# Down-weight sums of two pairs per layer, moved into the chunks by seven products; the order at the up-projections' ends

## The chip, the cores and the metric

One core of one Trainium2 chip. The metric is the device time of one execution, in microseconds; the kernel before has a median of 1107.97 us over three runs. Engines are named as in the profile: PE (TensorE), DVE (VectorE), ACT (ScalarE), POOL (GpSimd), SP (SyncE, which here only issues DMAs).

## The reference

A trunk of two layers over 512 positions of width 1024, all in float32:

```python
# layer 0: dilated attention, then the gated ConvFFN; one shared K, V and forget gate from the result
# layer 1: forgetting attention (FoX) over the shared K, V, then the gated ConvFFN
def conv_ffn(xn, w_up, cw, cb, w_down):
    a = xn @ w_up                         # 512 x 1024 times 1024 x 5632
    ap = jnp.pad(a, ((0, 0), (CONV_W - 1, 0), (0, 0)))
    a = sum(ap[:, j:j + T] * cw[j] for j in range(CONV_W)) + cb
    gate, val = jnp.split(a, 2, axis=-1)
    return (jax.nn.gelu(gate, approximate=True) * val) @ w_down   # 512 x 2816 times 2816 x 1024
```

## The kernel before

Every float32 product is made of three matmuls (`mm3`, L292 to L294: high by high, high by low, low by high). So each weight tile is needed as a pair: the high part is a rounding copy on ACT, the low part is the rest, by a subtraction on DVE or by a DMA that adds on POOL's queue. All instructions of an engine run in the order in which the program issues them.

**The course.** Attention of layer 0 to about 141 us, its output projection (141 to 182), ConvFFN of layer 0 (to 511), shared keys and values (511 to 611), FoX attention (611 to 727), its output projection (727 to 766), ConvFFN of layer 1 (764 to about 1100). The output projections are followed by a `Boundary`: for each block of 128 positions it normalises the product, adds it to the residual `h` (L337, L342, L344), normalises the sum for the next stage (L309) and transposes it (L360).

**ConvFFN, the up-projection.** 22 chunks c = 0..21 of 128 gate and 128 value columns. Chunks 3 to 20 (`SEVEN`) make their 2 x 2 block product by seven products instead of eight (a Strassen-like scheme): in order P1 = S2, P2 = S3, P3 = A12, P4 = S1, P5 = A22, then P0 = A11 of the next chunk (`open_seven`, its copy is L1002), P6 = S4. Each product is 12 matmuls of 256 columns. The weights of a chunk are made by a generator `seven_weights`, one part at each call of `step`: g0 and g1 the pair `a` (A11; L742, L744, then the adding DMA L745), g2 and g3 the pair `b` (A12 and A22; L748, L750, L751), g4 the sums on DVE and the high part of `u` (S2 and S1; L758, L759, L762), g5 that of `v` (S3 and S4; L764, L766), g6 and g7 the low parts of `u` and `v` (L771, L774). In chunk c, the chunk m = c+1 gets g4 to g7 and n = c+2 gets g0 to g3. After the products come the combining operations on the PSUM banks (copies L1028 `u2`, L1033 `s7`; additions L1038, L1042, L1043), and the convolution's taps (L678 on ACT, L682 on DVE), GELU (L706) and the gate's product (L701 on POOL, stored by L703). Chunks 2 and 21 take plain weights (`plain_weights`: L60 and L62 on ACT).

**Buffers.** The pool `t8` has 16 slots of 8 KB per partition, `t4` has 10 slots of 4 KB. A new tile takes a slot when the slot's last reader has finished. While the chunks by seven products run, 8 slots of `t8` hold the activations (`xsh`, `xsl` and the sums), the other 8 the pairs `a`, `b`, `u`, `v` of chunks c, m and n. `b` of chunk c is last read by P5, `u` by P4, `v` by P6.

**The down-projection.** 11 pairs of 256 rows. For each pair the kernel forms sums of the four quarters of the down weights and keeps them in DRAM (`dT`): `down_sums` loads a pair by three DMAs on SP (L642 to L644, 1 MB), makes four subtractions of 128 x 512 on DVE (L647 to L650) and stores 1 MB (L655). The sums of most pairs are made at other places, with these four among them: layer 0 pair 10 and layer 1 pair 8 in layer 0's output projection (from the function `late` and in the `Boundary`), layer 1 pair 10 in layer 1's output projection (`bd.beside`), and layer 1 pairs 9, 0 and 1 in the stage of the shared keys and values (`down1`). At the end of the up-projection the first pairs of the down-projection are prepared: `pair_sums(j)` (three DVE operations L809 to L811 on the gated activations, a store on POOL L812), `pair_highs(j)` (three ACT copies L819), `pair_lows(j)` (three DVE subtractions L824).

Of the kernel before, what the change touches and what calls it, by code (L numbers as in the profile page):

```python
# [13 lines left out]
ALU = mybir.AluOpType  # L14
# [7 lines left out]
NF = DFF // 128  # L22
# [5 lines left out]
SEVEN = tuple(range(3, 21))  # L28
# [80 lines left out]
def trunk_kernel(ctx, tc, x, norm_gains, w_qkv_a, w_o_a, w_q_b, w_o_b, kv_norm, w_kvf, b_f,  # L109
# [319 lines left out]
    class Boundary:  # L429
# [6 lines left out]
        def __init__(self, gain_mix, gain_next, name):  # L436
            self.mix, self.gain_next, self.name = Mix(gain_mix), gain_next, name
            self.xn, self.r, self.pts = {}, {}, {}
            self.xT, self.beside = None, iter(())

        def half(self, i, n, hf, o):
            b = self.order[i]
            self.mix.half(b, n, hf, o)
            if n == 0:
                if i >= 2:
                    self.transpose(self.order[i - 2])
                if i >= 1:
                    self.norm(self.order[i - 1])
                if i >= 2:
                    self.keep(self.order[i - 2])  # L450
                next(self.beside, None)
            else:
                self.mix.add(b)

# [177 lines left out]
    def down_sums(pairs, place, queue, lag, behind):  # L632


        live, n = [], len(pairs)
        for i in range(n + lag + behind):
            if i < n:
                l, j = pairs[i]
                a, b = place()
                live.append((a, b))  # L640
                r = w_down[l][j * 256:j * 256 + 256, :].rearrange("(c p) d -> c p d", p=128)
                sp.dma_start(a, r[0])  # L642
                sp.dma_start(b[:, 0:512], r[1, :, 512:1024])
                sp.dma_start(b[:, 512:1024], r[1, :, 0:512])  # L644
            if 0 <= i - lag < n:
                a, b = live[i - lag]
                dve.tensor_tensor(a[:, 0:512], a[:, 512:1024], a[:, 0:512], ALU.subtract)  # L647
                dve.tensor_tensor(a[:, 512:1024], b[:, 0:512], a[:, 512:1024], ALU.subtract)
                dve.tensor_tensor(b[:, 0:512], b[:, 0:512], a[:, 0:512], ALU.subtract)
                dve.tensor_tensor(b[:, 512:1024], b[:, 512:1024], b[:, 0:512], ALU.subtract)  # L650
            i -= lag + behind
            if i >= 0:
                l, j = pairs[i]
                for q, t in enumerate(live[i]):
                    queue[min(i, len(queue) - 1)].dma_start(dT[l][j, :, q * 1024:q * 1024 + 1024], t)  # L655
            yield

    def in_one():
# [13 lines left out]
    def ffn(l, bd, cp, nxt, ahead):  # L672
# [112 lines left out]
        def step(c, n=1):  # L785

            if c >= NF or c < 0:
                return
            if c not in gens:
                gens[c] = (seven_weights if c in SEVEN else plain_weights)(c)  # L790
            for _ in range(n):
                next(gens[c], None)
# [193 lines left out]
        step(S0, 4)  # L986
        for _ in split_sums():
            pass
        step(S0, 2)
        post(0, first[0:2])  # L990
        step(S0, 2)
        begun = opened = half_taps = None
        before = 1, first[2:4]

        def prod(o, w, x, start=False):
            half_mm(o, w, x[0:2], x[2], start)
# [8 lines left out]
        for c in range(2, NF):  # L1005
            if c == NF - 4:
                pair_load(0)
            m, n = c + 1, c + 2
            if c in SEVEN:
                x21, x22 = [(xT[0][i], xT[1][i], s) for i, s in ((1, LO), (1, HI))]  # L1010
                banks, s1 = opened
                opened = None
                w = halves.pop(c)
                W.n_get += 2
                o1, o2, o3, o4 = banks[0][:, LO], banks[0][:, HI], banks[1][:, LO], banks[1][:, HI]
                u2, s7 = (t2([128, 256], name="csum") for _ in range(2))
                prod(o2, w.pop("S2"), (*XB, HI))
                prod(o3, w.pop("S3"), (*XA, HI), True)
                product()
                bb = half_taps or t4([128, 2, T], name="bb")  # L1020
                cb, prev = before
                for i, ch in ((1, NF + cb), (0, cb)):
                    if i == 0 or half_taps is None:
                        first_tap(bb, i, prev[i], ch)
                        other_taps(bb, i, prev[i], ch)
                half_taps = None
                step(n)
                act.copy(u2, o2)  # L1028
                step(n)
                prod(o1, w.pop("A12"), x21)  # L1030
                prod(o2, w.pop("S1"), (*XA, LO))
                glu(cb, bb)
                act.copy(s7, o3)  # L1033
                if m in SEVEN:
                    step(m, 2)
                if n in SEVEN:
                    step(n)
                dve.tensor_tensor(o1, o1, s1, ALU.add)  # L1038
                if m in SEVEN:
                    step(m)  # L1040
                prod(o3, w.pop("A22"), (*XB, LO))
                dve.tensor_tensor(o4, o2, s7, ALU.add)  # L1042
                dve.tensor_tensor(o3, o3, u2, ALU.add)  # L1043
                if n in SEVEN:
                    step(n)
                half_taps = t4([128, 2, T], name="bb")
                first_tap(half_taps, 1, banks[1], NF + c)
                if m in SEVEN:
                    opened = open_seven(m)
                    step(m)  # L1050
                else:
                    begun = W.get(), bank([128, T], name="up")
                    up(*begun, range(4))
                    XA.clear()
                    XB.clear()
                    step(m)
                    pair_highs(0)
                    pair_sums(1)
                other_taps(half_taps, 1, banks[1], NF + c)
                prod(o2, w.pop("S4"), x22)  # L1060
            else:
                banks = [bank([128, T], name="up") for _ in range(2)]
                for s in range(2):
                    if s == 0 and begun:
                        w, banks[0] = begun
                        up(*begun, range(4, KD))
                        begun = None
                    else:
                        up(W.get(), banks[s], range(KD))
                    if s == 0 and m in SEVEN:  # L1070
                        opened = open_seven(m)
                        step(n, 2)
                    if s == 0:
                        post(*before, (lambda: pair_lows(0)) if c == NF - 1 else None, half_taps)
                        half_taps = None
                        if c >= NF - 2:
                            pair_highs(c - NF + 2)
                            pair_sums(c - NF + 3)
                    if n not in SEVEN:
                        step(n, 2 - s)  # L1080
                    elif s == 1:
                        step(n, 2)
            before = c, banks
            if c == NF - 3:
                pair_sums(0)
        post(*before, lambda: pair_lows(1))
        pair_highs(2)
        pair_sums(3)
        pair_lows(2)
# [360 lines left out]
    combine(1, 1)  # L1450
    weigh(2, 1)

    beside = down_sums([(0, ND - 1), (1, 8)], in_one, [sp], 2, 2)
    next(beside)
    next(beside)
    rows = load_conv(0)
    grow = t2([16, 128], name="g_rows")
    sp.dma_start(grow[0:8, :], kv_norm.rearrange("(k p) -> k p", p=128))
# [4 lines left out]
    def late():  # L1463
        combine(2, 0)
        combine(2, 1)
        cp.append(conv_columns(rows))
        pg = bank([128, 16], name="g_ps")
        pe.transpose(pg, grow, ident[:16, :16])
        dve.tensor_copy(gcol, pg)
        next(beside)  # L1470
        next(beside)

    bd = Boundary(load_gain(norm_gains[0, 1], "gain01"), load_gain(norm_gains[0, 2], "gain02"), "xb")
    bd.beside = beside
    Proj(6, 4, lambda kc: (OT[kc // 2][:, 0, kc % 2, :], OT[kc // 2][:, 1, kc % 2, :])).finish(bd, 4, late)


# [260 lines left out]
        keep_values(1, 2 + bp, vb[bp])  # L1738
        keep_values(1, bp, vd[bp])
    del w22, S4  # L1740
    down1 = down_sums([(1, j) for j in (9, 0, 1)], in_two, [pool, pool, sp], 1, 1)
    next(down1)
    W.ahead = 2
    W.split(W.n_split + 1)
    for bp in range(2):
# [4 lines left out]
                mm3(vc[bp], ah, al, w4[s][0][:, k, :], w4[s][1][:, k, :], False, False, True)  # L1750
        keep_values(0, bp, vc[bp])
    del w4
    next(down1)
    for c in range(4, 8):
        if c == 7:
            for i in range(4):
# [146 lines left out]
            W.split(W.n_get + 1)  # L1903
    f_bias(0, 0)
    f_bias(0, 1)
    M = len(pairs)
    sums, idle = {}, itertools.repeat(None)
    for j, m in ((2, 2), (3, 6), (4, 10), (5, 14)):
# [49 lines left out]
    W.ahead, W.ahead_dma = 4, 2  # L1958
    cp = conv_columns(load_conv(1))
    bd = Boundary(load_gain(norm_gains[1, 1], "gain11"), load_gain(norm_gains[1, 2], "gain12"), "xc")  # L1960
    bd.beside = down_sums([(1, ND - 1)], in_one, [sp], 1, 1)
    next(bd.beside)
    po.finish(bd, 4)


# [43 lines left out]
```

## Time and profile before

| | before |
|---|---|
| runs | 1106.59, 1108.63, 1107.97 us; median 1107.97 |
| the profiled execution | 1108.61 us, span 1106.8 us, mean granted clock 0.999 |
| busy in the span | PE 1086.2 us (98%), DVE 902.4 (82%), ACT 751.1 (68%), POOL 303.5 (27%) |
| moved by DMA | 250.02 MB, mean 226 GB/s |

A row of the timeline gives an instruction's start and duration in us, its engine and line, and in brackets the idle time of the engine just before it and what ended that. A row of the waits gives how long an engine stood idle for one kind of releaser in all, how many times, and the longest.

### The profile page before, as it was taken

The page shows a single profiled execution, that of the slowest core. Times are in us where ns is not written, and L with a number is a line of the kernel's source. Part 1 is how long each engine was busy: PE and PEld are TensorE (multiplying, and loading weights), DVE is VectorE, ACT ScalarE, POOL GpSimd, SP SyncE. Part 2 cuts the span into 40 slices and gives each one's busy share as a digit, 9 for nine tenths or more (in the row PEclk, how much of TensorE's full clock was granted, in tenths as well). Part 3 has the DMA queues.
Part 4 walks back from the last instruction along what each step waited for, and adds up shares of the span by engine and source line. Part 5 has one row for each costly group of instructions (what it writes and reads, how often), then busy time and mean ns, then how long its engine had stood idle before and what let it go on. Part 6 is the DMA issues. An engine that isn't in the chain of part 4 may idle for free. (4 is left out here: it accounts for less than half of the span.)

```text
span 1106.8 us, 19977 instructions
## 1 busy us (share of the span) xinstructions
PE 1086.2 (98%) x7184; PEld 964.4 (87%) x7184; DVE 902.4 (82%) x1494; ACT 751.1 (68%) x1290; POOL 303.5 (27%) x407
## 2 busy tenths in 40 slices
PE   9999999999999999999999899999999999999997
PEld 6988879999999988887987678788999999997886
DVE  5677788788888889997888677938789888879995
ACT  6644577688787766576554577756777887856573
POOL 4633010232333322000110566610133333321000
PEclk9999999999999999999999999999999999999999
DMA  9589997588888869793774676597688888879862
GB/s 315 128 287 408 372 271 192 130 216 206 210 214 209 212 218 367 264 339 77 210 176 128 192 234 204 156 306 198 144 195 216 210 203 208 214 216 354 313 248 76
DMA packets 192426, 250.02 MB, mean 226 GB/s; under 512 B 13696, under 2 KB 133496, under 8 KB 191816
## 3 DMA queue, kind: packets, MB, share of 16 engines
q1 hardware_dynamic: 169864, 180.81, 50.7%
q0 software_dynamic: 22464, 67.94, 27.2%
q8 instruction: 56, 0.92, 0.3%
q14 instruction: 42, 0.34, 0.1%
HBM read 170.28 MB, written 39.63 MB: 190 GB/s over the span
## 5 line engine op out<-in xcount | busy, mean ns | idle before, releaser
L292 PE MATMUL up<-xsh,w 128*128 128x256 f32 x576 | 163.2, 283 | 1.0 <-ACT csum L1002 1.0
L293 PE MATMUL up<-xsl,w 128*128 128x256 f32 x576 | 163.0, 283 | 0.0
L294 PE MATMUL up<-xsh,w 128*128 128x256 f32 x576 | 163.0, 283 | 0.0
L682 DVE SCALAR_TENSOR_TENSOR bb<-up,conv,bb 128x511 f32<-128x511 f32 (+1 forms) x160 | 119.3, 748 | 14.5 <-ACT bb L678 11.6
L292 PE MATMUL acc<-w 128*128 128x512 f32 (+1 forms) x311 | 120.5, 388 | 0.0
L294 PE MATMUL acc<-w 128*128 128x512 f32 (+1 forms) x311 | 120.4, 387 | 0.0
L292 PEld LDWEIGHTS up<-xsh,w 128*128 128x128 f32 x576 | 110.6, 192 | 1.4 <-ACT csum L1002 1.4
L293 PEld LDWEIGHTS up<-xsl,w 128*128 128x128 f32 x576 | 110.6, 192 | 0.1
L294 PEld LDWEIGHTS up<-xsh,w 128*128 128x128 f32 x576 | 110.6, 192 | 0.0
L293 PE MATMUL acc<-w 128*128 128x512 f32 (+1 forms) x267 | 103.7, 388 | 1.8 <-DVE w L824 1.8
L678 ACT ACTIVATE bb<-up,conv 128x512 f32<-128x512 f32 x80 | 62.1, 779 | 41.3 <-PE up L294 28.8
L751 POOL DMA_DIRECT2D w<-wraw x36 | 30.9, 858 | 166.9 <-ACT w L750 164.8
L60 ACT CAST w<-wraw 128x1024 fp32r<-128x1024 f32 x64 | 66.8, 1053 | 12.4 <-DMA wraw<-in_w_o_b_dram 4.2
L701 POOL TENSOR_TENSOR hc<-bb 128x512 f32<-128x512 f32 x44 | 68.9, 1567 | 0.1
L292 PEld LDWEIGHTS acc<-w 128*128 128x128 f32 x311 | 58.4, 188 | 12.0
L294 PEld LDWEIGHTS acc<-w 128*128 128x128 f32 x311 | 58.4, 188 | 11.8
L69 DVE TENSOR_TENSOR w<-wraw,w 128x1024 fp32r<-128x1024 f32 x44 | 54.3, 1243 | 10.7 <-ACT w L60 8.8
L762 ACT CAST w<-wsum 128x1024 fp32r<-128x1024 f32 x36 | 38.0, 1054 | 36.8 <-DVE wsum L759 36.8
L293 PEld LDWEIGHTS acc<-w 128*128 128x128 f32 x267 | 50.1, 188 | 13.5 <-DVE w L824 3.6
L292 PE MATMUL up<-xbh,w 128*128 128x256 f32 (+1 forms) x176 | 53.6, 304 | 0.5 <-ACT csum L1028 0.3
L292 PE MATMUL up<-xch,w 128*128 128x256 f32 (+1 forms) x176 | 53.5, 304 | 0.5 <-DVE up L1042 0.2
L824 DVE TENSOR_TENSOR w<-wraw,w 128x1024 fp32r<-128x1024 f32 x44 | 54.0, 1268 | 0.0
(344 smaller groups left out, 3476.5 us busy)
## 6 DMA issues: line engine op xcount, KB each, us to landing
wraw<-in_w_up_dram SPq DMA_DIRECT2D x144, 256.0 KB
w<-wraw POOLq DMA_DIRECT2D x56, 512.0 KB, 5.9
dT<-dsums SPq DMA_DIRECT2D x32, 512.0 KB
hD<-hc POOLq DMA_DIRECT2D x44, 256.0 KB, 5.0
dact<-hD SPq DMA_DIRECT2D x44, 256.0 KB
wraw<-dT SPq DMA_DIRECT2D x22, 512.0 KB
wraw<-in_w_down_dram SPq DMA_DIRECT2D x22, 512.0 KB
dsums<-in_w_down_dram SPq DMA_DIRECT2D x18, 512.0 KB
```

The source lines that it names most:

```text
L60: self.nc.scalar.copy(pair[:, 0, s], raw[:, s])
L69: self.nc.vector.tensor_tensor(pair[:, 1, s], raw[:, s], pair[:, 0, s].bitcast(F32), ALU.subtract)
L292: pe.matmul(o, ah, bh, start=first, stop=False, skip_group_check=shared)
L293: pe.matmul(o, ah, bl, start=False, stop=False, skip_group_check=shared)
L294: pe.matmul(o, al, bh, start=False, stop=last, skip_group_check=shared)
L678: act.activation(bb[:, i, :], ps, AF.Identity, bias=cp[:, 3, ch:ch + 1], scale=cp[:, 2, ch:ch + 1])
L682: dve.scalar_tensor_tensor(bb[:, i, n:], ps[:, :T - n], cp[:, 2 - n, ch:ch + 1], bb[:, i, n:], ALU.mult, ALU.add)
L701: pool.tensor_tensor(hc[c], bb[:, 0, :], bb[:, 1, :], ALU.mult)
L751: pool.dma_start(b[:, 1], r1, accum_op=ALU.add)
L762: act.copy(u[:, 0], sb)
L824: dve.tensor_tensor(w[:, 1], r, w[:, 0].bitcast(F32), ALU.subtract)
```

## The change

- `down_sums` of the pairs (0,10), (1,8) and (1,10) go from the output projections; the `Boundary` has no `beside` any more. `down1` makes two pairs, (1,0) and (1,1), instead of three, is begun later (after the last products of the shared values), and its last step comes after the first two biases of FoX.
- In each ConvFFN, a new generator `sums_beside` makes the sums of pairs (l,10) and (1,8+l). It is advanced once in each chunk by seven products, right ahead of the addition L1038: chunk 3 nothing, chunk 4 the three loads into one `t8` tile, chunks 5 to 8 one subtraction each, chunk 9 one store of 1 MB; then the same from chunk 10 to 15.
- The order of other steps: g0 to g3 of chunk 4 are made ahead of the loop, right behind the split of the activations' sums; where chunk n is not by seven products, its weights come after the copy `u2`; g2 (the copy L748 of `b`) stands behind P5 instead of ahead of L1038; at the end `pair_lows(1)` stands ahead of the last chunk's taps and `pair_sums(2)`, `pair_highs(2)` after them.

```diff
+    def sums_beside(*pairs):
+        yield
+        for l, j in pairs:
+            t = t8([128, 2, 1024], name="dsums")
+            a, b = t[:, 0], t[:, 1]
+            r = w_down[l][j * 256:j * 256 + 256, :].rearrange("(c p) d -> c p d", p=128)
+            sp.dma_start(a, r[0])
+            sp.dma_start(b[:, 0:512], r[1, :, 512:1024])
+            sp.dma_start(b[:, 512:1024], r[1, :, 0:512])
+            yield
+            dve.tensor_tensor(a[:, 0:512], a[:, 512:1024], a[:, 0:512], ALU.subtract)
+            yield
...
+            sp.dma_start(dT[l][j].rearrange("p (q d) -> p q d", q=2), t)
+            del t
             yield
...
         for _ in split_sums():
             pass
+        step(S0 + 1, 4)
         step(S0, 2)
...
+        beside = sums_beside((l, ND - 1), (1, 8 + l))
...
-                step(n)
+                if n in SEVEN:
+                    step(n)
                 act.copy(u2, o2)
-                step(n)
+                step(n, 1 if n in SEVEN else 2)
                 prod(o1, w.pop("A12"), x21)
                 prod(o2, w.pop("S1"), (*XA, LO))
                 glu(cb, bb)
                 act.copy(s7, o3)
                 if m in SEVEN:
                     step(m, 2)
-                if n in SEVEN:
-                    step(n)
+                next(beside, None)
                 dve.tensor_tensor(o1, o1, s1, ALU.add)
                 if m in SEVEN:
                     step(m)
                 prod(o3, w.pop("A22"), (*XB, LO))
+                if n in SEVEN:
+                    step(n)
                 dve.tensor_tensor(o4, o2, s7, ALU.add)
...
                         opened = open_seven(m)
-                        step(n, 2)
...
-                        if c >= NF - 2:
-                            pair_highs(c - NF + 2)
-                            pair_sums(c - NF + 3)
+                        if c == NF - 1:
+                            pair_highs(1)
                     if n not in SEVEN:
                         step(n, 2 - s)
-                    elif s == 1:
-                        step(n, 2)
...
-        post(*before, lambda: pair_lows(1))
+        pair_lows(1)
+        post(*before)
+        pair_sums(2)
         pair_highs(2)
...
-    beside = down_sums([(0, ND - 1), (1, 8)], in_one, [sp], 2, 2)
...
-    bd.beside = beside
...
-    down1 = down_sums([(1, j) for j in (9, 0, 1)], in_two, [pool, pool, sp], 1, 1)
-    next(down1)
...
     del w4
-    next(down1)
+    down1 = down_sums([(1, j) for j in range(2)], in_two, [pool, sp], 1, 1)
...
     f_bias(0, 0)
     f_bias(0, 1)
+    next(down1)
...
-    bd.beside = down_sums([(1, ND - 1)], in_one, [sp], 1, 1)
-    next(bd.beside)
```

More of the change, by code (lines that the diff above doesn't have):

```diff
@@ L438, in __init__ @@
             self.xn, self.r, self.pts = {}, {}, {}
-            self.xT, self.beside = None, iter(())
+            self.xT = None
         def half(self, i, n, hf, o):
@@ L450, in half @@
                     self.keep(self.order[i - 2])
-                next(self.beside, None)
             else:
@@ L655, in down_sums @@
                     queue[min(i, len(queue) - 1)].dma_start(dT[l][j, :, q * 1024:q * 1024 + 1024], t)
+            yield
[10 more added lines that the diff above has]
+            dve.tensor_tensor(a[:, 0:512], a[:, 512:1024], a[:, 0:512], ALU.subtract)
+            yield
+            dve.tensor_tensor(a[:, 512:1024], b[:, 0:512], a[:, 512:1024], ALU.subtract)
+            yield
+            dve.tensor_tensor(b[:, 0:512], b[:, 0:512], a[:, 0:512], ALU.subtract)
+            yield
+            dve.tensor_tensor(b[:, 512:1024], b[:, 512:1024], b[:, 0:512], ALU.subtract)
+            yield
+            sp.dma_start(dT[l][j].rearrange("p (q d) -> p q d", q=2), t)
+            del t
             yield
@@ L1451, in trunk_kernel @@
     weigh(2, 1)
-    beside = down_sums([(0, ND - 1), (1, 8)], in_one, [sp], 2, 2)
-    next(beside)
-    next(beside)
     rows = load_conv(0)
@@ L1469, in late @@
         dve.tensor_copy(gcol, pg)
-        next(beside)
-        next(beside)
     bd = Boundary(load_gain(norm_gains[0, 1], "gain01"), load_gain(norm_gains[0, 2], "gain02"), "xb")
-    bd.beside = beside
     Proj(6, 4, lambda kc: (OT[kc // 2][:, 0, kc % 2, :], OT[kc // 2][:, 1, kc % 2, :])).finish(bd, 4, late)
```

## The prediction

> **What bounds the kernel now.** I read the page first: the shares of the engines.
>
> ```profile
> span 1106.8 us, 19977 instructions
> ...
> PE 1086.2 (98%) x7184; PEld 964.4 (87%) x7184; DVE 902.4 (82%) x1494; ACT 751.1 (68%) x1290; POOL 303.5 (27%) x407
> ```
>
> PE is busy for 1086.2 of 1106.8 us, and the change takes no matmul away and adds none. So it can win only PE's waits, and lose only by new ones. The waits of PE come next (what it waited for, us in all, times, the longest):
>
> ```profile
> PE o_ps L1860 <- ACT pT L1847: 2.7, 2, 2.1
> PE acc L293 <- DVE w L824: 1.8, 4, 0.8
> PE xt_ps L360 <- DVE xn L309: 1.6, 1, 1.6
> PE acc L293 <- DVE w L69: 1.5, 1, 1.5
> PE q_ps L294 <- DMA w<-wraw: 1.3, 1, 1.3
> ...
> PE k_ps L294 <- DVE w L69: 1.0, 1, 1.0
> PE up L292 <- ACT csum L1002: 1.0, 2, 0.5
> PE up L292 <- ACT csum L1028: 0.5, 3, 0.2
> PE up L292 <- DVE up L1042: 0.3, 2, 0.2
> ```
>
> Each of these nine rows lies at a place that the change touches; together they are 11.7 us idle. A wait costs more than its idle time, which the timeline at the start of the chunks by seven products shows (start, duration, engine, line):
>
> ```profile
> 224.82 1.05 ACT L748 CAST w<-wraw 128x1024 fp32r<-128x1024 f32 x1
> ...
> 227.39 0.35 ACT L1002 COPY csum<-up 128x256 f32<-128x256 f32 x1
> ...
> 227.05 0.28 PE L294 MATMUL up<-xbh,w 128*128 128x256 f32 x1
> 227.80 0.39 PE L292 MATMUL up<-xsh,w 128*128 128x256 f32 x1 [0.47 <-ACT csum L1002]
> 228.02 0.28 PE L293 MATMUL up<-xsl,w 128*128 128x256 f32 x1
> ```
>
> Here PE starts 0.75 after the matmul before and the next one comes 0.22 later, where the cadence is 0.12 (rows of the next fence: 335.77 in P5, 12 matmuls to a product). That is 0.63 and 0.10 lost, 0.73 for an idle time of 0.47: **idle plus 0.26**, of which 0.10 falls behind the waiting matmul. I use this for every wait.
>
> The steady chunk comes last, since it runs 18 times in each layer:
>
> ```profile
> 335.04 1.04 ACT L748 CAST w<-wraw 128x1024 fp32r<-128x1024 f32 x1
> 335.99 1.05 ACT L750 ACTIVATE w<-wraw 128x1024 fp32r<-128x1024 f32 x1
> 337.11 0.78 ACT L678 ACTIVATE bb<-up,conv 128x512 f32<-128x512 f32 x1
> 337.80 0.36 ACT L1002 COPY csum<-up 128x256 f32<-128x256 f32 x1
> ...
> 334.65 0.43 DVE L1038 TENSOR_TENSOR up<-up,csum 128x256 f32<-128x256 f32 x1 [0.83 <-PE up L294]
> ...
> 335.77 0.28 PE L294 MATMUL up<-xsh,w 128*128 128x256 f32 x1
> ...
> 338.77 0.28 PE L292 MATMUL up<-xsh,w 128*128 128x256 f32 x1
> ```
>
> P5 ends at 335.77 + 0.28 = 336.05, P1 of the next chunk starts 2.72 later at 338.77, and the copy L1002 that it needs is done at 338.16: 0.61 to spare. No wait in the steady chunk, then, but little room on ACT between P5 and P1.
>
> **The change part by part.**
>
> *The subtractions in the chunks.* One of 128 x 512 takes 0.69 (rows below) and stands ahead of L1038, where DVE idles 0.83. It fits by 0.14; if L1038 slips by 0.1, P1 does not see it, since ACT's chain is later. Cost 0, and at most 0.1 for each of 16, 1.6, if the cover fails.
>
> *The tile of the sums.* The 1 MB tile takes a slot of `t8`. I count the slots when `b` of chunk n is made: 8 for activations, `b` and `v` of c, `a`, `b`, `u`, `v` of m, `a` of n, 15, so today `b`(n) is the 16th and takes the slot that `u`(c) left at P4's end. With the sums alive, `v`(m) takes `u`(c)'s slot, and the only one left for `b`(n) is that of `b`(c), free when P5 ends. So L748, which today starts 1.01 before P5's end (335.04 against 336.05), must wait for it. Behind it on ACT stand L750, L678 and L1002, in that order; PE waits for L1002, DVE for the tap L678, POOL's queue for L750. Of these only PE's is short. The length of the chain back to back is in the first timeline: from L748 at 224.82 to PE at 227.80, 2.98; with 0.06 of wake-up (227.39 + 0.35 to 227.80) it ends 3.04 after P5, 0.32 later than 2.72, and 0.10 is lost behind it: **0.42 for a chunk**. The tile lives through chunks 4 to 15; in 4 and 10 its loads come behind L748 and I take it that `b`(n) is served first. So 10 chunks in each of two layers: 20 x 0.42 = **+8.4**. Bounds: 0 if the slot comes free otherwise; 24 x 0.42 = 10.1 with chunks 4 and 10. That L748 also stands later in the order costs nothing by itself: no other instruction is between on ACT.
>
> *The DMAs.* In each layer six loads and two stores pass SP's queue in the chunks, 1 MB in and 1 MB out for a pair, one pair in six chunks (some 60 us): 33 GB/s on top of what the chunks move. They stand behind the chunk's weight loads; cost 0, at most that of the row on stores below.
>
> *Sums out of layer 0's projection.*
>
> ```profile
> 150.90 0.67 DVE L647 TENSOR_TENSOR dsums<-dsums 128x512 f32<-128x512 f32 x1
> ...
> 155.84 0.69 DVE L650 TENSOR_TENSOR dsums<-dsums 128x512 f32<-128x512 f32 x1
> 156.45 1.22 DVE L69 TENSOR_TENSOR w<-wraw,w 128x1024 fp32r<-128x1024 f32 x1
> ...
> 746.71 0.68 DVE L647 TENSOR_TENSOR dsums<-dsums 128x512 f32<-128x512 f32 x1
> ...
> 748.88 0.69 DVE L650 TENSOR_TENSOR dsums<-dsums 128x512 f32<-128x512 f32 x1
> ```
>
> Eight subtractions run from 150.90 to 156.53, and the weights' low part L69, for which PE waits 1.5, is queued behind them. Without them it is done some 5 us earlier. The wait goes: −(1.5 + 0.26) = **−1.75** (1.5 to 1.8).
>
> *Layer 1's projection.* Four subtractions, 746.71 to 749.57, stand within the norm of one block; without them L309 comes up to 2.9 earlier, and the wait of the transposes L360 of 1.6 goes: **−1.85** (1.6 to 2.1).
>
> *Chunk 4's weights ahead of the loop.*
>
> ```profile
> 202.74 1.05 ACT L762 CAST w<-wsum 128x1024 fp32r<-128x1024 f32 x1 [3.77 <-DVE wsum L759]
> ...
> 222.92 1.06 ACT L762 CAST w<-wsum 128x1024 fp32r<-128x1024 f32 x1 [0.97 <-DVE wsum L759]
> ...
> 380.91 1.06 ACT L62 ACTIVATE w<-wraw 128x1024 fp32r<-128x1024 f32 x1
> 381.87 0.36 ACT L1028 COPY csum<-up 128x256 f32<-128x256 f32 x1
> ```
>
> The four ACT operations (1.04 and 1.05 for L748 and L750, the two for `a` half as wide) move into an idle stretch of 3.77 before 202.74. They no longer stand in front of the taps in chunk 2. Per layer PE waits there three times (L1002 0.5, L1028 and L1042 0.2 each by the waits): 0.9 idle, about 1.6 whole. The last of them stays limited by ACT's chain from 222.92 to 227.74, which runs without idle time but starts at DVE's wsum, so I take half: −0.78 per layer, **−1.55** in all (0.8 to 3.2). Chunk 4's raw loads are taken earlier by the same step, behind no new wait on SP.
>
> *Plain weights behind `u2`.* In chunk 19, L1028 at 381.87 is queued behind L60 and L62 and PE waits for it 0.15 (third count of the row, 0.5 in 3). The new order ends that: idle plus 0.26, −0.42 per layer, **−0.85** (0 to 0.85).
>
> *The end of the up-projection.* Two waits per layer for L824 (1.8 in 4): 1.8 + 4 x 0.26 = 2.84. `pair_lows(1)` ahead of the taps is ready some 1.6 earlier, but DVE is full from there on, and the same work comes behind: I expect the lows of pair 2 to be late next by about 0.5 with 0.26, once per layer. So −0.98, hardly −1.42 or more: **−1.95** in all (0 to 2.8).
>
> ```profile
> 417.64 1.43 POOL L701 TENSOR_TENSOR hc<-bb 128x512 f32<-128x512 f32 x1
> ...
> 416.70 1.22 DVE L824 TENSOR_TENSOR w<-dact,w 128x1024 fp32r<-128x1024 f32 x1
> 417.83 3.45 DVE L824 TENSOR_TENSOR w<-wraw,w 128x1024 fp32r<-128x1024 f32 x2
> ```
>
> DVE is slower here beside POOL's L701: two L824 take 3.45, where two of 1.22 would take 2.4, so about 1 more. If the moved lows meet L701 where they did not before, the gain of this place is lost, a rival below. The Trainium skill, "SBUF — State Buffer", section "SBUF: two separate sides", has a rule for it: a DVE operation with two inputs in SBUF and a GpSimd operation that reads SBUF lock each other out of a shared pair of ports for a whole instruction. The row agrees (about 1 of the 1.43 is lost); by the rule a low that starts behind L701 waits for all of it, and the sum would be about −2 instead of −3.9.
>
> *Keys and FoX.*
>
> ```profile
> 604.69 1.22 DVE L69 TENSOR_TENSOR w<-wraw,w 128x1024 fp32r<-128x1024 f32 x1
> ...
> 610.73 2.50 SPq L1588 DMA_DIRECT2D ck<-cd  x2
> ...
> 618.37 0.73 POOL L1794 TENSOR_SCALAR bias<-ck,cq 128x128 f32<-128x128 f32 x2 [9.00 <-DMA ck<-cd]
> ```
>
> At 604.69 L69 stands behind four subtractions of a pair that now comes one step later: PE's wait of 1.0 goes, **−1.25** (1.1 to 1.25). The forget gates' load L1588 stands on SP at 610.73 behind two stores of sums, and POOL waits for it 9.00, to 618.37; from there DVE, ACT and PE's 2.1 at L1860 hang. Four subtractions less (2.8) ahead of the gates and the stores moved behind the biases bring it forward by about 2.7; then the longest wait, 2.1 + 0.26, is gone and of the one for the next weights (q_ps, 1.3) half of its 1.55: **−3.1** (1.0 to 3.9). POOL's store of the other pair stays behind the gates' own store, as now.
>
> *Sum.* 1.75 + 1.85 + 1.55 + 0.85 + 1.95 + 1.25 + 3.1 = 12.3 won, 8.4 lost: **−3.9**. Span 1106.8 to 1102.9; the profiled execution (1108.61, 0.06% above the median of 1107.97) to 1104.7; the median to **1104.1 us**, −0.35%.
>
> **The rivals.**
>
> *The wait for P5 does not come* (another slot is free, or ACT catches up): the gains alone, 1107.97 − 12.3 = 1095.7. For it: the 0.61 to spare covers more than half of the delay. Against: the count of slots, and 3.04 against 2.72.
>
> *The gains turn into the next waits.* At full DVE and DMA queues every wait may move. With the lower ends, 1.5 + 1.6 + 0.8 + 0.4 + 0 + 1.1 + 1.0 = 6.4, and 8.4 lost: 1110.0, hardly slower. For it: q_ps waits for a DMA, not for DVE.
>
> *The lows meet POOL:* the 1.95 at the end is lost, 1106.0.
>
> *The store holds the slot.* In chunks 9 and 15 the sums' tile is read by the store, which lands late:
>
> ```profile
> DMA to landing us min/median/max: 3.0/5.0/9.0
> ```
>
> (the row of `dT`'s DMAs). If `b`(n) there gets the slot of the sums and not `b`(c)'s, L748 waits for 334.65 + 5.0 = 339.65 instead of 336.1, 3.55 more, four times: +14.2, net +10.3, 1118.3, slower. It decides once the store's landing counts as the earlier release; P5 ends 1.4 after the store is issued, before any landing of 3.0, which speaks against it.
>
> **How the numbers follow.** Forecast 0.45 (own range 1101 to 1107), no wait for P5 0.17, gains turned 0.18, lows beside POOL 0.08, store 0.12. About 0.2% (2.2 us) is what a measurement of this kernel can tell from no change: faster means under 1105.75. Faster: 0.38 of the forecast, 0.17, 0.03: 0.58. Same: 0.07 + 0.05 + 0.10 = 0.22. Slower: 0.08 + 0.12 = 0.20. The range runs from the case without the wait, 1095.0 with its edge, to that of turned gains, 1110.5, and leaves out the store and some of the edges.
>
> **What would show it.** Right: PE waits for L1002 of about 0.16 idle in each of chunks 5 to 9 and 11 to 15, their period 10.50 instead of 10.08, and L748 idle until P5's last matmul; the waits for L69, L309, L1860 gone. Wrong: a period of 10.08 in all chunks (then the gains stand alone), or waits of several us in chunks 9 and 15 (the store), or the FoX wait at its old place, because the gates' load was held by the DMA queues and not by SP's order.

## The result

The changed kernel takes 1102.63 us (median of five runs, 1102.34 to 1103.21) where the kernel before takes 1107.97 (1106.59 to 1109.64 beside it): a ratio of 0.9952, 95% interval 0.9938 to 0.9967. That is 5.3 us less, where the forecast was 3.9 less. The two profiled executions, from which all that follows is read, lie 6.0 apart (spans of 1106.8 and 1100.8). First the changed kernel's page, the lines of the shares, one group of matmuls and its weight loads (busy, mean ns, then the idle time before them and what ended it):

```profile
span 1100.8 us, 19930 instructions
...
PE 1087.4 (99%) x7184; PEld 965.5 (88%) x7184; DVE 906.2 (82%) x1494; ACT 749.8 (68%) x1290; POOL 304.3 (28%) x405
...
L292 PE MATMUL up<-xsh,w 128*128 128x256 f32 x576 | 165.4, 287 | 3.9 <-ACT csum L1026 1.0
...
L292 PEld LDWEIGHTS up<-xsh,w 128*128 128x128 f32 x576 | 110.4, 192 | 8.4 <-ACT csum L1026 8.3
```

The same weight loads in the kernel before:

```profile
L292 PEld LDWEIGHTS up<-xsh,w 128*128 128x128 f32 x576 | 110.6, 192 | 1.4 <-ACT csum L1002 1.4
```

Most lines of the changed kernel are some 16 to 24 further down: L748 is now L770, L750 L772, L678 L700, L1002 L1026, L1038 L1062, L701 L723, L824 L846, L1860 L1876. All that PE waited for:

```profile
PE warm L259 <- DVE eps_t L254: 1.2, 1, 1.2
PE up L292 <- ACT csum L1026: 1.0, 2, 0.5
PE xt_ps L1329 <- DMA h<-in_x_dram: 0.9, 1, 0.9
PE acc L293 <- DVE w L846: 0.7, 4, 0.2
PE o_ps L1876 <- ACT pT L1863: 0.6, 1, 0.6
PE qk_ps L1357 <- ACT w L60: 0.3, 1, 0.3
```

Six of the nine rows shown of before are gone (L69 twice, L309, the DMA for q_ps, L1028, L1042); L824 is down from 1.8 to 0.7, L1860 from 2.7 to 0.6, and L1002's two at chunk 4 stand as they were. What is not in this list is the new wait in the chunks, and it is the largest: PE's queue of weight loads shows it on the page (8.3 us idle for L1026, 1.4 for L1002 before), and so does the matmuls' row, which has 3.9 us of idle time where the list names 1.0. The other 2.9 are 20 waits of 0.14 to 0.15 each, one at P1 in each of 20 chunks.

Both kernels issue the same 7184 matmuls in the same order, so each can be laid beside its counterpart. The difference of their start times, stage by stage (the measured column adds up to the 6.0 of the spans):

| stage | forecast | measured |
|---|---|---|
| layer 0's projection | -1.75 | -1.77 |
| start of the chunks, two layers | -1.55 | -0.72 - 0.71 |
| chunks 4 to 15, two layers | +8.4 | +3.96 + 3.95 |
| chunk 19, two layers | -0.85 | -0.37 - 0.40 |
| start of the down-projection, two layers | -1.95 | -0.56 - 0.54 |
| keys | -1.25 | -1.24 |
| FoX | -3.1 | -4.88 |
| layer 1's projection | -1.85 | -2.02 |
| the kernel's first loads and its last 10 us | 0 | -0.7 |

The steady chunk of the changed kernel, chunk 8 of layer 0, ACT, then PE:

```profile
272.99 1.05 ACT L788 CAST w<-wraw 128x1024 fp32r<-128x1024 f32 x1 [0.41 <-PE up L294]
274.43 1.05 ACT L770 CAST w<-wraw 128x1024 fp32r<-128x1024 f32 x1 [0.39 <-PE up L294]
275.38 1.05 ACT L772 ACTIVATE w<-wraw 128x1024 fp32r<-128x1024 f32 x1
276.34 0.76 ACT L700 ACTIVATE bb<-up,conv 128x512 f32<-128x512 f32 x1
277.00 0.36 ACT L1026 COPY csum<-up 128x256 f32<-128x256 f32 x1
...
274.11 0.28 PE L294 MATMUL up<-xsh,w 128*128 128x256 f32 x1
...
277.41 0.39 PE L292 MATMUL up<-xsh,w 128*128 128x256 f32 x1
277.64 0.28 PE L293 MATMUL up<-xsl,w 128*128 128x256 f32 x1
```

P5's last matmul ends at 274.11 + 0.28 = 274.39; only then does L770 start, and everything behind it on ACT runs back to back to 277.36. P1 starts at 277.41, 3.02 after P5's end (2.72 before), and its second matmul 0.23 later instead of 0.12: 0.30 and 0.11. The period, from P1 to P1, is 10.48 in chunks 4 to 8 and 10 to 14 (10.38 in chunk 10) and goes back to 10.08 from chunk 16 on.

### The profile page after: what moved, and what is told of

Same layout as the page of the kernel before. It is cut to its first block, busy times and chain, and to the rows that moved or that the text cites. A ratio compares the mean times of both kernels' runs of the same rounds, so it can differ in the third digit from the quotient of the medians.

```text
span 1100.8 us, 19930 instructions
## 1 busy us (share of the span) xinstructions
PE 1087.4 (99%) x7184; PEld 965.5 (88%) x7184; DVE 906.2 (82%) x1494; ACT 749.8 (68%) x1290; POOL 304.3 (28%) x405
## 5 line engine op out<-in xcount | busy, mean ns | idle before, releaser
L700 ACT ACTIVATE bb<-up,conv 128x512 f32<-128x512 f32 x80 | 61.5, 772 | 24.5 <-PE up L294 14.6
L723 POOL TENSOR_TENSOR hc<-bb 128x512 f32<-128x512 f32 x44 | 68.7, 1560 | 22.8 <-ACT bb L728 14.5
L69 DVE TENSOR_TENSOR w<-wraw,w 128x1024 fp32r<-128x1024 f32 x44 | 54.5, 1252 | 10.4 <-ACT w L60 10.2
L846 DVE TENSOR_TENSOR w<-wraw,w 128x1024 fp32r<-128x1024 f32 x44 | 56.2, 1317 | 0.0
```

What stands on the lines that cost most here:

```text
L69: self.nc.vector.tensor_tensor(pair[:, 1, s], raw[:, s], pair[:, 0, s].bitcast(F32), ALU.subtract)
L700: act.activation(bb[:, i, :], ps, AF.Identity, bias=cp[:, 3, ch:ch + 1], scale=cp[:, 2, ch:ch + 1])
L723: pool.tensor_tensor(hc[c], bb[:, 0, :], bb[:, 1, :], ALU.mult)
L846: dve.tensor_tensor(w[:, 1], r, w[:, 0].bitcast(F32), ALU.subtract)
```

## Experiments

The theory: the tile of the sums takes the 16th slot, `b`'s copy waits for P5 and ACT's chain behind it for P1; what is won is won at the old places of the sums and by the order. The rival for the chunks: the added subtraction, the DMAs or the new order of the copy itself make the 0.4.

**b's low part behind P0's copy.**

```diff
                 dve.tensor_tensor(o3, o3, u2, ALU.add)
-                if n in SEVEN:
-                    step(n)
...
                     opened = open_seven(m)
+                    if n in SEVEN:
+                        step(n)
```

> The changed kernel with one step moved: g3 (the copy L772 of b's low part and its adding DMA) is issued behind the copy L1026 of P0 instead of ahead of the tap L700. The slot and ACT theory: b's copy L770 still waits for P5's last matmul, but only L770, L700 and L1026 then stand between P5 and P1, so L1026 ends about 0.95 earlier, 0.6 ahead of P1's need; every chunk takes 10.08 again, and the 8.2 us of the waits are won: 1102.6 - 8.2 = 1094.4. The rival that the added DVE subtraction or the transfers make the 0.4 per chunk: periods of 10.48 stay, 1102.6.

1094.28, ratio 0.9876 (0.9863 to 0.9890), and 1094.00 in a second job. ACT in the steady chunk, and P1:

```profile
252.54 1.05 ACT L770 CAST w<-wraw 128x1024 fp32r<-128x1024 f32 x1 [0.39 <-PE up L294]
253.56 0.78 ACT L700 ACTIVATE bb<-up,conv 128x512 f32<-128x512 f32 x1
254.24 0.36 ACT L1026 COPY csum<-up 128x256 f32<-128x256 f32 x1
254.49 1.07 ACT L772 ACTIVATE w<-wraw 128x1024 fp32r<-128x1024 f32 x1
...
255.22 0.28 PE L292 MATMUL up<-xsh,w 128*128 128x256 f32 x1
```

L770 still waits for P5 (0.39 of idle time, as above), but L1026 ends at 254.60, 0.62 before P1. The matmuls laid beside those of before lose nothing in the chunks of layer 0 and 0.2 in those of layer 1. The subtractions, the DMAs and the slot are all as they were: the chain's length on ACT was the price. That the time met its expectation is in part luck: 7.7 us came in the chunks, and 1.2 at the wait for L1026 at chunk 4's P1 (the two of 0.5 in the list above), which the expectation didn't count and which also goes; 0.4 was lost at the kernel's first loads.

**Two subtractions in a chunk.**

```diff
             dve.tensor_tensor(a[:, 0:512], a[:, 512:1024], a[:, 0:512], ALU.subtract)
-            yield
             dve.tensor_tensor(a[:, 512:1024], b[:, 0:512], a[:, 512:1024], ALU.subtract)
             yield
             dve.tensor_tensor(b[:, 0:512], b[:, 0:512], a[:, 0:512], ALU.subtract)
-            yield
             dve.tensor_tensor(b[:, 512:1024], b[:, 512:1024], b[:, 0:512], ALU.subtract)
```

> The changed kernel with two subtractions in a chunk instead of one, so that the tile of the sums lives through fewer chunks (loads in chunk 4, subtractions in 5 and 6; the second pair two chunks sooner as well). The slot theory: waits of P1 in the chunks while the tile lives, 4 to 6 and 8 to 10 or so, 6 of a layer instead of 10; 8 x 0.41 = 3.3 won: 1099.3; that two subtractions (1.38) do not fit DVE's idle 0.83 costs nothing, since L1062 has room to PE. The rival that the subtractions themselves cost: the same number of them and less cover, 1102.6 or more, with longer periods in chunks 5 and 6.

1099.99, ratio 0.9930 (0.9918 to 0.9943). It is 0.7 above its expectation. Laid beside the changed kernel's matmuls it wins 1.5 in the chunks of each layer, some 0.4 for each of the four in which the tile is dead now. So the wait follows the tile's life and not the number of subtractions; that two of them run in one gap of DVE costs nothing.

**All sums at their old places, the new order kept** (`sums_beside` out, the three calls of `down_sums` of before in).

> All sums at their old places (projections and shared keys and values), none in the chunks; all of the new order, with b's copy behind P5. Theory: without a 16th live tile the copy does not wait, all chunks take 10.08 (8.2 won), and the waits at the old places return as the traces show them (projection 0: 1.77, keys 1.24, FoX about 4.6, projection 1: 2.0; 9.6 in all): 1102.6 + 1.4 = 1104.0. The rival that the new order of b's copy makes the chunks' waits: periods of 10.48 stay, 1112.

1105.24, ratio 0.9980 (0.9970 to 0.9989): the new order alone makes the kernel before about 2 us faster. Its chunks take 10.08, with `b`'s copy ahead of P5's end again though it stands behind P5 in the order:

```profile
333.00 1.04 ACT L789 CAST w<-wraw 128x1024 fp32r<-128x1024 f32 x1
333.95 1.04 ACT L771 CAST w<-wraw 128x1024 fp32r<-128x1024 f32 x1
...
334.68 0.28 PE L294 MATMUL up<-xsh,w 128*128 128x256 f32 x1
```

P5 ends at 334.68 + 0.28 = 334.96, and L771 starts 1.01 before that with no idle time ahead of it, so the new order costs nothing; the slot does. The time came out 1.2 above its expectation. Its profiled span is 2.0 above the changed kernel's instead of 1.4: FoX lost 5.0 and not 4.6 (next), the chunks won 7.9 and not 8.2, the first projection lost 1.8 and the second 1.6 and not 2.0, and 0.4 came behind the last matmul. The other 0.6 is not found in the trace; its runs spread from 1104.3 to 1106.2.

**Pair 9 of layer 1 back in the keys and values.**

```diff
-        beside = sums_beside((l, ND - 1), (1, 8 + l))
+        beside = sums_beside(*((l, ND - 1), (1, 8 + l))[:2 - l])
...
+    down1 = down_sums([(1, j) for j in (9, 0, 1)], in_two, [pool, pool, sp], 1, 1)
+    next(down1)
...
-    down1 = down_sums([(1, j) for j in range(2)], in_two, [pool, sp], 1, 1)
+    next(down1)
...
     f_bias(0, 1)
-    next(down1)
```

> Only pair 9 of layer 1 goes back to its old place in the keys and values (three pairs there, at the old points of the program), so layer 1's chunks carry one pair. Theory: the keys' wait (1.24) and the two FoX waits with what hangs on them (4.6) return, and five waits of 0.41 in layer 1's chunks go: 1102.6 + 5.8 - 2.1 = 1106.4. The rival that FoX won by something else (an earlier start, other transfers): 1102.6 - 2.1 + 1.2 = 1101.8.

1106.69, ratio 0.9993 (0.9984 to 1.0002). Beside the changed kernel it loses 1.24 at the keys and 4.45 in FoX and wins 2.0 in layer 1's chunks. These three numbers are the price of the pair together with the old places of the stage's steps, which this run brings back too. FoX's loss is 0.5 at the scores ahead of the wait of before (o_ps), 2.3 at that wait, and 1.6 in the windows behind it, which look like this (span of the window, its length, busy us of PE, PEld, DVE, ACT and POOL, then the granted clock, the DMA engines' share and GB/s):

```profile
628.00:630.00 2.00, 0.93 (x10) 0.69 (x12) 1.97 (x6) 1.46 (x5) 1.93 (x5) 0.94 1.01 269
630.00:632.00 2.00, 2.00 (x10) 1.38 (x7) 1.80 (x12) 1.71 (x8) 1.47 (x3) 0.50 1.08 230
632.00:634.00 2.00, 2.00 (x11) 1.59 (x10) 0.83 (x4) 0.82 (x4) 0.15 (x1) 0.71 0.28 53
634.00:636.00 2.00, 2.00 (x14) 1.69 (x12) 0.65 (x1) 0.87 (x3) 1.93 (x4) 1.00 0.00 0
```

The clock falls to 0.50 behind the wait of 2.09, for 3.4 us (more on this in the last section), and matmuls of 512 columns come every 0.43 instead of 0.23. In this kernel that takes the place of the wait for q_ps's weights, which land meanwhile. The same happens with the sums at their old places.

**The gates' load behind the stores.**

```diff
     next(down1)
+    next(down1)
     load_ck(0)
...
     f_bias(0, 1)
-    next(down1)
```

> The changed kernel with the last step of the two pairs in the keys and values (the stores of the second on SP) issued ahead of the load of the forget gates' sums instead of behind the first two biases. The theory that SP's order set FoX's start: the stores wait for the subtractions (done at 614.6), the load goes out at about 614.9 instead of 607.2 and lands at 620.7, PE's wait at L1876 is longer than in the kernel before: 1102.6 + 6 = 1108.6, or 1.4 more if the clock falls in the wait. The rival that only the subtractions on DVE held the gates back: 1102.6, with the first bias at 612.9.

1109.36, ratio 1.0022 (1.0012 to 1.0031), so this one call alone costs 6.7. That is between the two numbers expected without and with a fall of the clock; the profiled execution (1109.58) has such a fall. The load on SP and the first bias on POOL, first in the changed kernel, then with the stores ahead:

```profile
607.15 0.33 SPq L1606 DMA_DIRECT2D ck<-cd  x1
613.05 1.89 SPq L654 DMA_DIRECT2D dT<-dsums  x2
...
612.91 1.14 POOL L1810 TENSOR_SCALAR bias<-ck,cq 128x128 f32<-128x128 f32 x2 [4.36 <-DMA ck<-cd]
```

```profile
613.09 1.78 SPq L654 DMA_DIRECT2D dT<-dsums  x2
614.97 1.23 SPq L1606 DMA_DIRECT2D ck<-cd  x2
...
621.50 0.72 POOL L1811 TENSOR_SCALAR bias<-ck,cq 128x128 f32<-128x128 f32 x2 [12.92 <-DMA ck<-cd]
```

The load goes out 7.8 later and the bias starts 8.6 later, so a wait in SP's order can set FoX's start. In the change itself SP's order is the smaller part. The load needs the gates' sums, which POOL stores, first in the kernel before, then in the changed one:

```profile
607.77 0.52 POOL L1569 DMA_DIRECT2D cd<-c  x1 [22.25 <-DVE c L1568]
```

```profile
605.23 0.56 POOL L1587 DMA_DIRECT2D cd<-c  x1 [39.61 <-DVE c L1586]
```

This store went out 2.5 earlier, behind four subtractions less on DVE, and the load followed it by 1.9 (607.15) instead of 3.0 (610.73): 1.0 is SP's order. The first bias starts 5.5 earlier (612.91 for 618.37), so that 1.9 more lies between the load's issue and the bias, and no run isolates that part.

**The old order at the end of the up-projections, and the old place of chunk 4's weights.** Each undone alone.

```diff
-                        if c == NF - 1:
-                            pair_highs(1)
+                        if c >= NF - 2:
+                            pair_highs(c - NF + 2)
+                            pair_sums(c - NF + 3)
...
-        pair_lows(1)
-        post(*before)
-        pair_sums(2)
+        post(*before, lambda: pair_lows(1))
```

> The changed kernel with the old order at the up-projections' end alone (the lows of pair 1 behind the first taps of the last chunk, the highs and sums of pair 2 ahead). Theory: the two waits of 0.76 and 0.17 idle per layer return (1.47 whole) and the two of about 0.2 that came for the lows of pair 2 (0.90 whole) go: 2 x 0.57 = 1.1 more than the changed kernel, 1103.7. The rival that the order at the end gives nothing, because DVE is full there: 1102.6.

1103.71, ratio 0.9969 (0.9957 to 0.9980). The two waits of before return (0.90 + 0.11 and 0.34 + 0.11 at the matmuls), the two for the lows of pair 2 go: 0.53 per layer.

```diff
-        step(S0 + 1, 4)
         step(S0, 2)
...
+                        step(n, 2)
...
+                    elif s == 1:
+                        step(n, 2)
```

> The changed kernel with the weights of chunk 4 made within chunk 2 again instead of ahead of the loop. Theory: ACT's taps of chunk 2 stand behind these copies again, the waits of 0.15 and 0.16 idle return and the one at P1 of chunk 4, together 0.74 per layer: 1102.6 + 1.5 = 1104.1. The rival that the earlier part of the chunk gives it back, since ACT's chain to L1026 sets P1 of chunk 4 either way: under 0.4 in both layers together, 1102.9.

1104.13, ratio 0.9973 (0.9962 to 0.9984): 1.5 above the changed kernel. By the matmuls it is 0.7 in each layer, at the two waits ahead of chunk 4's P1.

**What holds the down-projection's start.** On top of the kernel with `b`'s low part behind P0's copy: once `pair_lows(2)` ahead of `pair_sums(3)`, once the last gate product on DVE.

> The kernel with g3 behind P0's copy, and at the up-projections' end the lows of pair 2 ahead of the sums of pair 3. Theory: these lows come 1.3 earlier, the two waits for L846 (0.90 whole per layer) go: 1094.3 - 1.8 = 1092.5. The rival that the lows then meet POOL's L723 for longer, or that the sums of pair 3 are late in their place: 1094.3 or more.

1094.95, ratio 0.9889 (0.9875 to 0.9902), no gain. The waits moved on to the lows of pair 3 (1.8 in 4 instead of 0.8 in 4). The lows of pair 2 now wait for ACT's high parts of the same pair (L841), and a small operation of DVE's met POOL's product in their place:

```profile
413.32 1.23 DVE L846 TENSOR_TENSOR w<-dact,w 128x1024 fp32r<-128x1024 f32 x1 [1.11 <-ACT w L841]
...
418.44 0.42 DVE L832 TENSOR_TENSOR dact<-dact 128x256 f32<-128x256 f32 x1
418.90 1.62 DVE L833 TENSOR_TENSOR dact<-dact 128x256 f32<-128x256 f32 x1
...
418.93 1.30 POOL L723 TENSOR_TENSOR hc<-bb 128x512 f32<-128x512 f32 x1
```

Its 0.42 became 1.62: the loss, 1.20, is POOL's instruction but for 0.1. The Trainium skill, "SBUF — State Buffer", section "SBUF: two separate sides", has a DVE operation with two inputs in SBUF and a GpSimd operation that reads SBUF lock each other out for a whole instruction, and this row agrees. This loss only takes the place of the 1.1 that the two L846 lost beside the product before; what makes the lows of pair 3 later is the 1.11 of idle time ahead of L846.

```diff
         pair_lows(2)
-        product()
+        product(dve)
```

> The kernel with g3 behind P0's copy, and the last gate product of each layer (hc of chunk 21, L723) made on DVE behind the lows of pair 2 instead of on POOL, where it ran beside them (two L846 took 3.45 there, 2.35 elsewhere). The theory of the mutual wait of DVE and POOL: the two L846 take 2.35, the lows are 1.1 earlier, the waits of PE for them (0.90 whole per layer) go, the 0.69 on DVE is paid from the 1.1: 1094.3 - 1.8 = 1092.5. The rival that DVE is full anyway and the wait moves on to the lows of pair 3, as it did with the lows put ahead: 1094.3 to 1095.

1091.69, ratio 0.9860 (0.9843 to 0.9877), beside this on the same chip:

> The kernel with g3 behind P0's copy once more, for a comparison on one chip with the kernel whose last gate product is on DVE: 1094.3 beside 1107.6 of the kernel before, with the same two waits for L846 per layer.

1094.00, ratio 0.9881 (0.9861 to 0.9902). In the changed kernel the two L846 beside POOL's product took 3.45; here they and the product take

```profile
414.67 2.35 DVE L846 TENSOR_TENSOR w<-wraw,w 128x1024 fp32r<-128x1024 f32 x2
416.94 0.69 DVE L723 TENSOR_TENSOR hc<-bb 128x512 f32<-128x512 f32 x1
```

and no wait of PE for L846 is left. By the matmuls that is 0.96 in each layer, 1.9 of the 2.3 us between the two medians. It is the fastest kernel of this study, 16 us under the kernel before.

## Why the prediction was right, step by step

**The slot and ACT's chain** stood as forecast, 0.40 a chunk for 0.42 and ten chunks a layer. Which ten was wrong: the copies held are those of chunks 4 to 8 and 10 to 14, not 5 to 9 and 11 to 15. I had the loads of chunks 4 and 10 behind L748, but in the changed kernel they stand ahead of L1062 and its copy L770 stands behind P5, so the tile takes the slot that `u`(c) leaves at P4's end in chunk 4, and `b`(n) waits from that chunk on. The store is out sooner than its place in the program, chunk 9: SP sends it 2.7 behind the last subtraction, still in chunk 8:

```profile
231.09 0.35 SPq L664 DMA_DIRECT2D dsums<-in_w_down_dram  x1
...
275.54 0.50 SPq L676 DMA_DIRECT2D dT<-dsums  x1
```

That also decides the rival of the store that holds the slot: I priced the store as issued at L1062's place in chunk 9, but it is out about 8 earlier. The sign that I named, a wait of about 0.16 idle for the copy at each of these P1, is in the trace: 0.14 to 0.15 each, at P1 of chunks 5 to 9 and 11 to 15, and with 0.41 lost for each the rule of idle plus 0.26 holds once more. Only the list of waits leaves them out; the start times, the two rows of the page and L770's own idle time show them.

**The two projections, the keys, the plain weights and chunk 4's weights** came within 0.2 of their terms. At chunk 4 I had taken half of three waits; the two small ones went and the one at P1 stayed whole. The plain weights' part is read from the traces alone, no run takes that step back by itself.

**FoX was mis-sized**, -3.1 for -4.88. I took half of the wait for q_ps's weights as lasting; it went whole (-1.55). At the wait of o_ps and the scores just ahead of it 2.7 went for 2.36, and 0.5 more came at later steps of FoX, whose cause no run here isolates. I had the load 2.7 earlier; it was 3.6, and the bias behind it 5.5. The chain itself, from SP's load over POOL's bias, is what the moved stores and the restored pair confirm.

**The end of the up-projections was mis-sized the other way**, -1.10 for -1.95. For the most part that is a slip in my sum: its own parts, 1.42 won and 0.76 lost in each layer, make -1.3 and not -1.95, and the forecast with them -3.3 and not -3.9. The rest is the late wait. I expected one late wait for the lows of pair 2 in each layer; both of their pieces came late, 0.9 for 0.75. The cause was in a row that I had quoted: the 3.45 beside POOL's product stays in the new order, and taking the product away takes the waits away. The rival named for this place, lows that meet POOL where they did not before, is not what happened: those of pair 2 met it in both kernels, and they are late now because PE comes to them sooner.

**The rival that the gains turn into the next waits** came true at this one place only.

**The total** is in part luck: FoX gave 1.8 more than its term and the first loads and the end of the kernel 0.7, the end of the up-projections 0.85 less (0.6 of it the slip), and the rest nearly met its terms. That is 2.1 in the traces and 1.4 in the medians.

## What to carry to other kernels

Before a buffer is added to a full pool, count which reader's end the next tile then waits for, and add up what stands behind that tile's first writer on its engine to the next thing the bound engine needs; moving one operation out of that stretch (b's low part, 1.05 us) gave back 8 us here, 7.7 of them in the chunks where the buffer lives. Work taken off a place where it delays a small load or a chain's head can be worth far more than its own duration: one call's place on SP's queue was 6.7 us. Small repeated waits may be absent from the list of waits; look for idle time on the page that the list doesn't name, and compare the matmuls' start times between two kernels.

## What was not expected of the hardware

After a wait of PE of 2.09 us at FoX's start the granted clock fell to 0.50 for 3.4 us in two kernels (the sums at their old places, and pair 9 back), and 1.6 us were lost there. Behind an equal wait in the kernel before it stayed at 1.00, and in the kernel with the gates' load behind the stores it fell behind a wait of 3.7. The traces tell the cases apart. In each of the twelve profiled executions the granted clock, once it has first risen, changes only after whole multiples of 3.413 us: 182 and 183 of them up to the falls in the two kernels, then one at 0.50. Cut into windows of that length and phase, the three kernels look like this around the wait, the kernel before first, then the old places, then pair 9:

```profile
623.59:627.00 3.41, 2.62 (x20) 1.83 (x18) 3.41 (x11) 3.08 (x7) 2.54 (x5) 1.00 0.51 137
627.00:630.41 3.41, 1.98 (x16) 1.44 (x17) 3.34 (x13) 2.56 (x10) 3.26 (x7) 1.00 0.79 187
630.41:633.83 3.42, 2.14 (x13) 1.50 (x12) 2.14 (x9) 2.34 (x9) 0.71 (x3) 1.00 0.65 140
```

```profile
623.68:627.09 3.41, 1.27 (x19) 0.83 (x17) 3.34 (x10) 3.05 (x10) 3.26 (x8) 1.00 0.75 159
627.09:630.50 3.41, 3.41 (x15) 2.40 (x10) 2.77 (x15) 1.86 (x8) 1.66 (x3) 0.50 1.08 248
```

```profile
626.33:629.75 3.42, 1.29 (x19) 0.85 (x17) 3.35 (x12) 3.13 (x10) 3.27 (x7) 1.00 0.93 223
629.75:633.16 3.41, 3.41 (x15) 2.40 (x12) 2.84 (x15) 1.86 (x8) 1.72 (x4) 0.50 0.88 190
```

In the kernel before the edge at 627.00 cuts the wait in two, PE is busy for 2.62 and 1.98 in the two windows, and the clock stays. In the other two the wait lies within one window, PE is busy for 1.27 and 1.29 in it, and the next window has half the clock. Over the whole windows of the twelve executions, some 320 in each, every one with PE busy for 1.29 or less was followed by one at 0.50, and none with 1.75 or more; where between the two the limit lies, no run shows. So what decides is how the wait falls into the windows, and these begin elsewhere in each execution. In 37 of 44 further executions of the kernel before the mean granted clock was 0.998 or less, for 0.999 in the profiled one, so the fall may be the common case there too; no trace of those shows it. The Trainium skill, "TensorE: Matmul & The Clock Gate", section "What's actually happening", has the clock halved after an idle window of about 3.4 us, and the window run free of the kernel. The free window of that length agrees with these traces; a whole idle window was not needed, since PE was busy for 1.29 of one that halved the clock.
